# Two inputs of one stage laid side by side in DRAM: the first projection block of a hybrid mLSTM block

## Chip, cores, metric

The kernel runs on 1 core of one Trainium2 chip. The metric is the device time of one execution in microseconds (us). For the kernel before, 985.32 us is the median of 3 runs (985.29 to 987.55).

## What is computed

One layer of an encoder on x of shape (256 tokens, 2048 channels), float32. Cut to what matters here:

```python
h    = x * rsqrt(mean(x*x) + eps) * norm_pre_w
proj = h @ w_in                                   # 2048 x 16400, split into eleven parts:
q, k, v, o_g, z_a, i_pre, f_pre, u_b, z_b, g_a, g_b = split(proj)
# A: causal conv on q and k, SiLU, chunkwise mLSTM with 8 heads, per-head RMSNorm, gates o_g and z_a
# B: window means of u_b (windows 2, 4, 8, 16) minus u_b, a 256 x 256 map per group, gate z_b
merged = sigmoid(g_a) * (y_a @ w_proj_mlstm) + sigmoid(g_b) * (y_b @ w_proj_pool)
x + rmsnorm(merged @ w_out) * norm_post_w
```

## The kernel before, in words

All of it is matrix products on TensorE (PE) in a split precision: ScalarE (ACT) rounds a float32 tile to a high part (`hi`), VectorE (DVE) subtracts to get the low part (`lo`), and PE adds up hi·hi, lo·hi and hi·lo. The helper `hi_lo` (L56 to L65) issues both; L59 and L60 are the plain pair, L62 and L63 the pair that also multiplies by a scale per partition.

Weights stream from DRAM once. `w_tile` (L96) takes a 1 MB tile `raw` (128 partitions x 2048 floats, four k tiles of 512 columns), from the pool `rawp`, which has **three** such buffers for the whole kernel; SyncE (SP) issues the load, and `hi_lo` splits it into halves `wh`, `wl` (pool `split`, four of each). `tok_block` (L110) then multiplies: for each k tile of 128 channels, x's hi and lo (in `xc`, L89) stand still in PE, for two groups of 128 tokens, and 512 columns of `wh` or `wl` move: 6 matmuls per k tile, 96 in a block of 16 k tiles. `chan_block` (L131) does the same with the weights standing still; its matmuls are L142 and L144.

The change concerns the **first block** (`pu` of L410 with b = 0, the first 512 columns of u_b). Here x itself has still to be loaded and split, so the block is run with `first` (L207), which gives `w_tile` other cuts and a function `pre` that is called ahead of each cut. x lies in DRAM transposed (`xT`), with the norm weight ahead of it, as 16 floats per partition. For the first four k tiles (kq = 0) one k tile at a time comes, x by a transfer of 128 KB (136 KB with the norm weights) at L219 and the weights by one of 256 KB at L104; for the other twelve, two k tiles at a time, 256 KB of x and 512 KB of weights. x's tiles are `xt0` and two buffers `xt`, apart from `rawp`; a `raw` holds four k tiles of weights. All these transfers are in SP's queue, x and weights in turn.

Behind the first block stand, in the program: `stats` (L226), which loads x again by rows into two `raw` buffers (L231; called x0 and x1 below), squares and sums it on ACT (L232), from which DVE (L191) and GpSimd (POOL, L192) make `rstd`; `pooling` (L340), whose first step scales the block's result by `rstd` (`u_h`, `u_l`, L62 and L63); `stats_bc` (L237), which makes a diagonal matrix of `rstd` (`dg`, L241) and multiplies it by ones on PE (L242); and the block of z_b with two tiles `in_wq` (L100; t0 and t1 below). These are generators that `tok_block` and `chan_block` step once per half tile, and a scheduler orders each engine's instructions. `gates` loads `gw` (L249) and splits it into `gc` (L59 and L60).

Of the kernel before, what the change touches and what calls it, by code (L numbers as in the profile page):

```python
# [36 lines left out]
def block_kernel(ctx: ExitStack, tc: tile.TileContext, a: dict, out: bass.AP):  # L37
# [55 lines left out]
    def xl(k, t):  # L93
        return xc[:, k, 1, t * P : (t + 1) * P]

    def w_tile(src, cuts=(0, 1024, 2048), pre=None, pool=split):  # L96

        raw = rawp.tile([P, 2048], F32, name="raw")
        if pre is None:
            nc.sync.dma_start(raw, src)  # L100
        for c0, c1 in zip(cuts, cuts[1:]):
            if pre is not None:
                pre(c0)
                nc.sync.dma_start(raw[:, c0:c1], src[:, c0:c1])  # L104
            wh = pool.tile([P, 1024], F32R, name="wh")
            wl = pool.tile([P, 1024], F32R, name="wl")
            hi_lo(wh[:, : c1 - c0], wl[:, : c1 - c0], raw[:, c0:c1])
            yield c0, c1, wh, wl

    def tok_block(tiles, st_h, st_l, opts=lambda kq: {}):  # L110

        ps = [acc.tile([P, 512], F32, name="acc") for _ in range(2)]
        n = 4 * len(tiles)
        for kq, src in enumerate(tiles):
            for c0, c1, wh, wl in w_tile(src, **opts(kq)):
                for part in range(2):
# [12 lines left out]
        return ps
# [20 lines left out]
    def xtiles(b):  # L150
        return [a["wx"][b, i].rearrange("p k c -> p (k c)") for i in range(4)]
# [50 lines left out]
    pool_ctx = ExitStack()  # L202
    ph2 = pool_ctx.enter_context(tc.tile_pool(name="ph2", bufs=1, side="right"))
    sp = pool_ctx.enter_context(tc.tile_pool(name="start", bufs=1))
    xt0 = sp.tile([P, KT + 4 * T], F32, name="xt0")

    def first(kq):  # L207


        xt = xt0 if kq == 0 else sp.tile([P, KT + 4 * T], F32, name="xt", bufs=2)  # L210
        xk = xt[:, KT:].rearrange("p (k t) -> p k t", k=4)
        cuts = (0, 512, 1024, 1536, 2048) if kq == 0 else (0, 1024, 2048)

        def pre(c0):
            k0, k1 = c0 // 512, min(cc for cc in cuts if cc > c0) // 512
            s0, s1 = KT + k0 * T, KT + k1 * T
            if kq == 0 and k0 == 0:
                s0 = 0
            nc.sync.dma_start(xt[:, s0:s1], a["xT"][:, kq * 4 * T + s0 : kq * 4 * T + s1])  # L219
            for kk in range(k0, k1):  # L220
                k = kq * 4 + kk
                hi_lo(xc[:, k, 0], xc[:, k, 1], xk[:, kk], xt0[:, k : k + 1])

        return {"cuts": cuts, "pre": pre}

    def stats():  # L226

# [179 lines left out]
        yield 1  # L407

    for b in range(2):
        pu = tok_block(xtiles(12 + b), xh, xl, *([first] if b == 0 else []))  # L410
        if b == 0:
            side.append(gates())
        side.append(pooling(b, pu, zbs))
        for g in range(2 * b, 2 * b + 2):
            side.append(pool_gate(chan_block(qtiles(16 + g))))
# [157 lines left out]
    def st(tile_):  # L573
        return lambda k, t: tile_[:, k, t * P : (t + 1) * P]
# [138 lines left out]
def _per_channel(v):  # L713
    return v.reshape(-1, P).T
# [54 lines left out]
```

## Time and profile before

| | |
|---|---|
| median of 3 runs | 985.32 us |
| the profiled execution | 985.57 us, of it 983.8 us span |
| PE busy | 972.0 us (99%) |
| DVE, ACT busy | 626.5 us (64%), 481.7 us (49%) |
| moved by DMA | 188.45 MB, mean 192 GB/s |
| GB/s in the first three 24.6 us slices | 318, 320, 216 |

The span runs from the first to the last instruction. A group in the views has a line of the kernel, an engine, an operation and its tiles (out<-in). In a timeline, the first column is the start in us from the span's start, the second how long the row lasts, `x8` says how many instructions are in it, and the bracket gives the engine's idle time before it and what ended it. A matmul's duration overlaps the next one's; the distance between starts is what it costs. `SPq` rows are the issuing of a transfer, not the transfer.

### The profile page before, as it was taken

What the parts mean: (1) busy time and instruction counts of PE and PEld (TensorE: products, weight loads), DVE (VectorE), ACT (ScalarE), POOL (GpSimd) and SP (SyncE); (2) the same over time, 40 slices, a digit from 0 to 9 for tenths busy, and PEclk for the clock granted to TensorE, in tenths of its full rate; (3) what the DMA queues carried; (4) which work ended last, traced back from release to release, by engine and by line L of the source; (5) the groups of instructions that cost most, each with busy time, mean ns of one, the idle gap of its engine ahead of it and who ended that gap; (6) DMA issues with size and microseconds to landing.
All of it is one profiled execution on the core that took longest, in us unless ns stands there. A gap on an engine that the chain in (4) does not pass through costs nothing.

```text
span 983.8 us, 12219 instructions
## 1 busy us (share of the span) xinstructions
PE 972.0 (99%) x4777; PEld 819.4 (83%) x4777; DVE 626.5 (64%) x886; ACT 481.7 (49%) x614; POOL 14.3 (1%) x31
## 2 busy tenths in 40 slices
PE   9999999999999999999999999999999999999996
PEld 6788888888888888888888888888888888888886
DVE  7688747767767768668677586454454455454563
ACT  6746444446644465446544465434434434443451
POOL 1000000000000000000000000000000000000001
PEclk9999999999999999999999999999999999999999
DMA  9854455545364445464454554555556555567542
GB/s 318 320 216 171 152 191 194 192 160 188 130 244 178 172 171 176 167 219 166 171 191 168 199 194 149 196 194 192 189 173 212 187 198 177 209 236 272 181 166 86
DMA packets 29017, 188.45 MB, mean 192 GB/s; under 512 B 3232, under 2 KB 4000, under 8 KB 7200
## 3 DMA queue, kind: packets, MB, share of 16 engines
q1 hardware_dynamic: 28528, 184.53, 53.0%
q10 hardware_dynamic: 432, 3.15, 0.8%
q8 instruction: 37, 0.61, 0.2%
q14 instruction: 20, 0.16, 0.0%
HBM read 185.57 MB, written 2.10 MB: 191 GB/s over the span
## 4 chain that ended last, share of the span: by engine, by line
PE 96%; issue 1%; DMA 1%; ACT 0%; SPq 0%; POOL 0%; DVE 0%; DVEq 0%; ACTq 0%; POOLq 0%
PE acc L122 23%; PE acc L123 23%; PE acc L125 23%; PE acc L142 15%; PE acc L144 8%; PE sm L69 1%; PE sm L70 1%; PE sm L68 1%; DMA raw<-in_wx 1%; PE acc L68 0%; PE acc L70 0%; PE acc L69 0%; PE sm L266 0%; PE sm L579 0%; PE sm L533 0%
## 5 line engine op out<-in xcount | busy, mean ns | idle before, releaser
L60 DVE TENSOR_TENSOR wl<-raw,wh 128x1024 fp32r<-128x1024 f32 (+1 forms) x338 | 407.5, 1217 | 257.8 <-ACT wh L59 257.0
L59 ACT CAST wh<-raw 128x1024 fp32r<-128x1024 f32 (+1 forms) x338 | 350.8, 1046 | 393.0 <-PE acc L123 275.0
L122 PE MATMUL acc<-wh,xc 128*128 128x512 f32 x704 | 276.6, 393 | 1.0 <-ACT wh L59 1.0
L123 PE MATMUL acc<-wh,xc 128*128 128x512 f32 x704 | 274.7, 390 | 0.0
L125 PE MATMUL acc<-wl,xc 128*128 128x512 f32 x704 | 188.7, 389 | 0.0
L142 PE MATMUL acc<-xc,wh 128*128 128x512 f32 x640 | 160.7, 393 | 1.2 <-ACT wh L59 1.2
L122 PEld LDWEIGHTS acc<-wh,xc 128*128 128x128 f32 x704 | 132.5, 188 | 28.6 <-ACT wh L59 2.7
L125 PEld LDWEIGHTS acc<-wl,xc 128*128 128x128 f32 x704 | 132.2, 188 | 27.8
L123 PEld LDWEIGHTS acc<-wh,xc 128*128 128x128 f32 x704 | 132.6, 188 | 26.3
L142 PEld LDWEIGHTS acc<-xc,wh 128*128 128x128 f32 x640 | 115.9, 189 | 22.8 <-ACT wh L59 1.4
L144 PEld LDWEIGHTS acc<-xc,wl 128*128 128x128 f32 x640 | 87.3, 190 | 6.3
L144 PE MATMUL acc<-xc,wl 128*128 128x256 f32 x640 | 89.2, 282 | 0.0
L122 PE MATMUL acc<-wh,y_h 128*128 128x512 f32 x128 | 49.8, 389 | 0.0
L123 PE MATMUL acc<-wh,y_l 128*128 128x512 f32 x128 | 49.8, 389 | 0.0
L451 DVE SCALAR_TENSOR_TENSOR cy<-pad,vec,cy 128x256 f32<-128x256 f32 x96 | 39.4, 481 | 0.0
L122 PE MATMUL acc<-wh,m_h 128*128 128x512 f32 x96 | 37.6, 391 | 0.0
L123 PE MATMUL acc<-wh,m_l 128*128 128x512 f32 x96 | 37.4, 389 | 0.0
L125 PE MATMUL acc<-wl,y_h 128*128 128x512 f32 x128 | 34.2, 389 | 0.0
L393 DVE TENSOR_REDUCE pad<-acc 128x256 f32<-128x512 f32 x32 | 20.6, 686 | 14.6 <-PE acc L144 14.6
L123 PEld LDWEIGHTS acc<-wh,y_l 128*128 128x128 f32 x128 | 24.0, 188 | 5.0
L125 PEld LDWEIGHTS acc<-wl,y_h 128*128 128x128 f32 x128 | 24.0, 188 | 5.0
L122 PEld LDWEIGHTS acc<-wh,y_h 128*128 128x128 f32 x128 | 24.0, 188 | 5.0
(188 smaller groups left out, 757.2 us busy)
## 6 DMA issues: line engine op xcount, KB each, us to landing
raw<-in_wx SPq DMA_DIRECT2D x84, 1024.0 KB, 4.8
raw<-in_wq SPq DMA_DIRECT2D x40, 1024.0 KB, 4.8
raw<-in_wpm SPq DMA_DIRECT2D x16, 1024.0 KB, 4.9
raw<-in_wo SPq DMA_DIRECT2D x16, 1024.0 KB, 5.0
raw<-in_wpp SPq DMA_DIRECT2D x8, 1024.0 KB, 4.8
raw<-in_wx SPq DMA_DIRECT2D x6, 512.0 KB, 6.9
raw<-in_x SPq DMA_DIRECT2D x2, 1024.0 KB, 7.7
xr<-in_x ACTq DMA_DIRECT2D x2, 1024.0 KB, 7.1
```

The source lines that it names most:

```text
L59: nc.scalar.copy(hi, src)
L60: nc.vector.tensor_tensor(lo, src, hi.bitcast(F32), op=ALU.subtract)
L68: nc.tensor.matmul(ps, lh, rh, start=start, stop=False)
L69: nc.tensor.matmul(ps, ll, rh, start=False, stop=False)
L70: nc.tensor.matmul(ps, lh, rl, start=False, stop=stop)
L122: nc.tensor.matmul(ps[t], st_h(k, t), wh[:, cols], start=k == 0, stop=False)
L123: nc.tensor.matmul(ps[t], st_l(k, t), wh[:, cols], start=False, stop=False)
L125: nc.tensor.matmul(ps[t], st_h(k, t), wl[:, cols], start=False, stop=k == n - 1)
L142: nc.tensor.matmul(ps[c], wh[:, cols], xc[:, k], start=k == 0, stop=False)
L144: nc.tensor.matmul(ps[c][:, 1], wl[:, cols], xc[:, k, 0], start=False, stop=k == KT - 1)
L393: nc.vector.tensor_reduce(dst, ps.rearrange("p a b -> p b a"), axis=AX.X, op=ALU.add)
L451: nc.vector.scalar_tensor_tensor(y, pad[:, 1 + j : 1 + j + T], cw[:, j : j + 1], y, op0=ALU.mult, op1=ALU.add)
```

## The change

x (256 floats per partition and k tile) and the weights of the first block (512 floats) are put side by side in one DRAM array `xw`, 3 KB per partition and k tile, the norm weights ahead of them as before. A transfer brings x and weights of one k tile, one k tile, two k tiles, and from then on of two at a time: 384, 384 and 768 KB. Only the first k tile comes in two transfers (136 KB with x, 256 KB with weights) into a buffer of its own, `xw0`. All others go into `raw` buffers, of which a transfer of two k tiles fills three quarters. The two buffers `xt` are gone. `w_tile` loses its options. The block's columns leave the array `wx`, whose later blocks move up by one.

```diff
+XW = T + 512
...
-    def w_tile(src, cuts=(0, 1024, 2048), pre=None, pool=split):
+    def w_tile(src, pool=split):
 
         raw = rawp.tile([P, 2048], F32, name="raw")
-        if pre is None:
-            nc.sync.dma_start(raw, src)
-        for c0, c1 in zip(cuts, cuts[1:]):
-            if pre is not None:
-                pre(c0)
-                nc.sync.dma_start(raw[:, c0:c1], src[:, c0:c1])
+        nc.sync.dma_start(raw, src)
+        for c0, c1 in ((0, 1024), (1024, 2048)):
...
-    def tok_block(tiles, st_h, st_l, opts=lambda kq: {}):
+    def tok_block(tiles, st_h, st_l, load=w_tile):
...
-            for c0, c1, wh, wl in w_tile(src, **opts(kq)):
+            for c0, c1, wh, wl in load(src):
...
-    xt0 = sp.tile([P, KT + 4 * T], F32, name="xt0")
+    xw0 = sp.tile([P, KT + XW], F32, name="xw0")
 
     def first(kq):
-        xt = xt0 if kq == 0 else sp.tile([P, KT + 4 * T], F32, name="xt", bufs=2)
-        xk = xt[:, KT:].rearrange("p (k t) -> p k t", k=4)
-        cuts = (0, 512, 1024, 1536, 2048) if kq == 0 else (0, 1024, 2048)
-
-        def pre(c0):
-            k0, k1 = c0 // 512, min(cc for cc in cuts if cc > c0) // 512
-            s0, s1 = KT + k0 * T, KT + k1 * T
-            if kq == 0 and k0 == 0:
-                s0 = 0
-            nc.sync.dma_start(xt[:, s0:s1], a["xT"][:, kq * 4 * T + s0 : kq * 4 * T + s1])
-            for kk in range(k0, k1):
-                k = kq * 4 + kk
-                hi_lo(xc[:, k, 0], xc[:, k, 1], xk[:, kk], xt0[:, k : k + 1])
-
-        return {"cuts": cuts, "pre": pre}
+        for k0, n in ((0, 1), (1, 1), (2, 2)) if kq == 0 else ((0, 2), (2, 2)):
+            c0 = KT + (kq * 4 + k0) * XW
+            if c0 == KT:
+                for s0, s1 in ((0, KT + T), (KT + T, KT + XW)):
+                    nc.sync.dma_start(xw0[:, s0:s1], a["xw"][:, s0:s1])
+                raw = xw0[:, KT:]
+            else:
+                raw = rawp.tile([P, 2048], F32, name="raw")[:, : n * XW]
+                nc.sync.dma_start(raw, a["xw"][:, c0 : c0 + n * XW])
+            r = raw.rearrange("p (k c) -> p k c", k=n)
+            wh = split.tile([P, 1024], F32R, name="wh")
+            wl = split.tile([P, 1024], F32R, name="wl")
+            w = [p[:, : n * 512].rearrange("p (k c) -> p k c", k=n) for p in (wh, wl)]
+            for kk in range(n):
+                k = kq * 4 + k0 + kk
+                hi_lo(xc[:, k, 0], xc[:, k, 1], r[:, kk, 0:T], xw0[:, k : k + 1])
+            hi_lo(*w, r[:, :, T:XW])
+            yield k0 * 512, (k0 + n) * 512, wh, wl
...
-        pu = tok_block(xtiles(12 + b), xh, xl, *([first] if b == 0 else []))
+        pu = tok_block(range(4), xh, xl, first) if b == 0 else tok_block(xtiles(12), xh, xl)
...
-        "xT": np.concatenate(
-            [_per_channel(g["norm_pre_w"][0]), x.reshape(T, KT, P).transpose(2, 1, 0).reshape(P, KT * T)], axis=1
-        ),
+        "xw": np.concatenate([_per_channel(g["norm_pre_w"][0]), xw.reshape(P, KT * XW)], axis=1),
```

In SP's queue at the start of the program, before: x and weights in turn; from row to row only the DMAHW numbers (transfers that must have landed) and one DVE wait tell when a row may go.

```order
L219 DMA xt_129<-in_xT 128x272
L104 DMA raw<-in_wx 128x512
...
L219 DMA xt<-in_xT 128x512 [waits DMAHW0_49]
L104 DMA raw<-in_wx 128x1024 [waits DMAHW1_49]
...
L219 DMA xt<-in_xT 128x512 [waits DMAHW2_49,DMAHW0_49,DVE_49]
L104 DMA raw<-in_wx 128x1024 [waits DMAHW1_49]
...
L100 DMA raw<-in_wq 128x2048 [waits DMAHW4_49,DVE_49]
L249 DMA gw<-in_wg 128x256 [waits DMAHW5_49]
...
L231 DMA raw<-in_x 128x2048 [waits DMAHW0_49,DVE_49]
L231 DMA raw<-in_x 128x2048 [waits DMAHW3_49,DMAHW1_49,DVE_49]
```

The same queue in the changed kernel (`in_xw` is the joint array; rows of the first block in order k tile 0 in two transfers, 1, 2 and 3, 4 and 5, ...):

```order
L211 DMA xw_129<-in_xw 128x272
L211 DMA xw_129<-in_xw 128x512
L215 DMA raw<-in_xw 128x768
L215 DMA raw<-in_xw 128x1536 x2
L215 DMA raw<-in_xw 128x1536 [waits DMAHW2_49,DVE_49]
L249 DMA gw<-in_wg 128x256
L215 DMA raw<-in_xw 128x1536 [waits DMAHW3_49,DVE_49]
L215 DMA raw<-in_xw 128x1536 [waits DMAHW4_49,DMAHW0_49,DVE_49]
...
L100 DMA raw<-in_wq 128x2048 [waits DMAHW0_49,DVE_49]
L252 DMA vec<-in_vecs 128x184
L231 DMA raw<-in_x 128x2048 [waits DMAHW6_49,DMAHW1_49,DVE_49]
L231 DMA raw<-in_x 128x2048 [waits DMAHW3_49,DVE_49]
```

Twenty rows of the first block have become ten; five go without a wait, and every later one waits for DVE, which has to be done with the `raw` buffer that the row fills again. The load of `gw` has moved from behind t0 (`in_wq`) into the block.

On ACT the splitting of `gw` has moved too. In the changed kernel it stands between the pieces for k tiles 6 and 7 and those for 8 and 9 (`xc` is x's part, `wh` the weights'):

```order
L63 ACTIVATE xc<-raw,xw_129 128x256 [waits DMAHW5_49]
L63 ACTIVATE xc<-raw,xw_129 128x256
L60 CAST wh<-raw 128x1024 [waits DVE_49,PE_49]
L60 CAST gc<-gw 128x4x2x8 [waits DMAHW6_49]
L60 CAST gc<-gw 128x4x2x8 x3
L63 ACTIVATE xc<-raw,xw_129 128x256 [waits DMAHW7_49]
```

Before, it stood behind the first block and both halves of t0, just ahead of the squares of x0. Otherwise ACT's, DVE's and PE's instructions are the same ones in the same order, with k tiles 2 and 3 now taken together on all three.

## Rows read from the trace of the kernel before

**Rows 1.** The page's part 1: busy us of each engine, its share of the span, and its instructions.

```profile
PE 972.0 (99%) x4777; PEld 819.4 (83%) x4777; DVE 626.5 (64%) x886; ACT 481.7 (49%) x614; POOL 14.3 (1%) x31
```

**Rows 2.** The waits of PE in the whole span, those for data: line waited for, us in total, times, longest.

```profile
PE acc L142 <- ACT wh L59: 1.2, 1, 1.2
PE acc L122 <- ACT wh L59: 1.0, 2, 0.8
```

**Rows 3.** Timeline of PE at the start: the warm-up matmuls, then first matmuls of k tiles 1, 2, 3, of the pairs 4 and 5, 6 and 7, and 8 and 9.

```profile
1.19 4.02 PE L165 MATMUL sm<-zeros 128*128 128x512 bf16 x9 [1.19 <-DVE zeros L160]
...
7.16 0.39 PE L122 MATMUL acc<-wh,xc 128*128 128x512 f32 x1
...
8.52 0.39 PE L122 MATMUL acc<-wh,xc 128*128 128x512 f32 x1
...
10.30 0.50 PE L122 MATMUL acc<-wh,xc 128*128 128x512 f32 x1 [0.26 <-ACT wh L59]
...
12.74 0.50 PE L122 MATMUL acc<-wh,xc 128*128 128x512 f32 x1 [0.77 <-ACT wh L59]
...
15.59 0.39 PE L122 MATMUL acc<-wh,xc 128*128 128x512 f32 x1
...
18.31 0.39 PE L122 MATMUL acc<-wh,xc 128*128 128x512 f32 x1
```

**Rows 4.** Timeline of PE behind the first block: start of t0, its last group, the two diagonal products, start of t1.

```profile
29.19 1.98 PE L142 MATMUL acc<-xc,wh 128*128 128x512 f32 x8
...
33.80 1.11 PE L144 MATMUL acc<-xc,wl 128*128 128x256 f32 x8
35.54 0.71 PE L242 MATMUL sm<-dg,ones_f 128*128 128x128 f32 x4 [0.63 <-DVE dg L241]
37.45 2.12 PE L142 MATMUL acc<-xc,wh 128*128 128x512 f32 x8 [1.20 <-ACT wh L59]
```

**Rows 5.** Timeline of ACT in the same stretch.

```profile
27.12 0.68 ACT L59 CAST gc<-gw 128x64 fp32r<-128x64 f32 x4
28.19 1.92 ACT L232 ACTIVATE raw<-raw 128x2048 f32<-128x2048 f32 x1 [0.39 <-DMA raw<-in_x]
...
32.17 1.92 ACT L232 ACTIVATE raw<-raw 128x2048 f32<-128x2048 f32 x1 [1.97 <-DMA raw<-in_x]
33.99 0.18 ACT L232 ACTIVATION_READ_ACCUMULATOR raw<-raw 128x1 f32 x1
35.20 1.26 ACT L62 ACTIVATE u_h<-acc,rstd 128x512 fp32r<-128x512 f32 x2 [1.02 <-POOL rstd L192]
36.35 4.11 ACT L59 CAST wh<-raw 128x1024 fp32r<-128x1024 f32 x4
```

**Rows 6.** Timeline of DVE: the low part of the last pair of k tiles, 14 and 15, of the first block.

```profile
23.80 1.22 DVE L60 TENSOR_TENSOR wl<-raw,wh 128x1024 fp32r<-128x1024 f32 x1 [1.23 <-ACT wh L59]
```

**Rows 7.** Timeline of ACT at the start: weights of k tile 0, x of k tile 1, x and weights of k tiles 4 and 5.

```profile
4.44 0.62 ACT L59 CAST wh<-raw 128x512 fp32r<-128x512 f32 x1 [0.95 <-DMA raw<-in_wx]
4.97 0.50 ACT L62 ACTIVATE xc<-xt 128x256 fp32r<-128x256 f32 x1
...
10.27 0.91 ACT L62 ACTIVATE xc<-xt,xt 128x256 fp32r<-128x256 f32 x2
11.64 1.05 ACT L59 CAST wh<-raw 128x1024 fp32r<-128x1024 f32 x1 [0.46 <-DMA raw<-in_wx]
```

**Rows 8.** Timeline of SP's issues: x and weights of k tile 0, weights of k tile 3, weights of 10 and 11, then x0 (the x2 row merges it with x1), and x1 alone.

```profile
0.74 0.39 SPq L219 DMA_DIRECT2D xt<-in_xT  x1
1.18 0.42 SPq L104 DMA_DIRECT2D raw<-in_wx  x1
...
4.01 0.43 SPq L104 DMA_DIRECT2D raw<-in_wx  x1
...
9.62 0.33 SPq L104 DMA_DIRECT2D raw<-in_wx  x1
...
19.79 5.59 SPq L231 DMA_DIRECT2D raw<-in_x  x2
25.06 0.33 SPq L231 DMA_DIRECT2D raw<-in_x  x1
```

**Rows 9.** DMA issues taken one at a time by narrow stretches: KB, and us from the start of the issue to landing. In order: the six issues of the group before (0.74, 1.18, 4.01, 9.62, 19.79 and 25.06 us), and the load of `pw` at 39.95 us, when little else was on its way.

```profile
xt<-in_xT SPq DMA_DIRECT2D x1, 136.0 KB, 2.2
raw<-in_wx SPq DMA_DIRECT2D x1, 256.0 KB, 3.2
raw<-in_wx SPq DMA_DIRECT2D x1, 256.0 KB, 5.6
raw<-in_wx SPq DMA_DIRECT2D x1, 512.0 KB, 7.7
raw<-in_x SPq DMA_DIRECT2D x1, 1024.0 KB, 8.4
raw<-in_x SPq DMA_DIRECT2D x1, 1024.0 KB, 7.0
raw<-in_pw SPq DMA_DIRECT2D x1, 1024.0 KB, 4.7
```

**Rows 10.** Busy time by stretch (us PE, PEld, DVE, ACT, POOL; then granted clock, DMA share, GB/s), 4 to 8 us.

```profile
4.00:6.00 2.00, 2.00 (x5) 0.94 (x4) 0.92 (x3) 1.03 (x2) 0.00 (x0) 1.00 0.95 260
6.00:8.00 2.00, 2.00 (x9) 1.62 (x9) 1.28 (x4) 1.72 (x4) 0.00 (x0) 1.00 1.07 295
```

More of the change, by code (lines that the diff above doesn't have):

```diff
@@ L94, in xl @@
         return xc[:, k, 1, t * P : (t + 1) * P]
-    def w_tile(src, cuts=(0, 1024, 2048), pre=None, pool=split):
+    def w_tile(src, pool=split):
         raw = rawp.tile([P, 2048], F32, name="raw")
-        if pre is None:
-            nc.sync.dma_start(raw, src)
-        for c0, c1 in zip(cuts, cuts[1:]):
-            if pre is not None:
-                pre(c0)
-                nc.sync.dma_start(raw[:, c0:c1], src[:, c0:c1])
+        nc.sync.dma_start(raw, src)
+        for c0, c1 in ((0, 1024), (1024, 2048)):
             wh = pool.tile([P, 1024], F32R, name="wh")
             wl = pool.tile([P, 1024], F32R, name="wl")
-            hi_lo(wh[:, : c1 - c0], wl[:, : c1 - c0], raw[:, c0:c1])
+            hi_lo(wh, wl, raw[:, c0:c1])
             yield c0, c1, wh, wl
-    def tok_block(tiles, st_h, st_l, opts=lambda kq: {}):
+    def tok_block(tiles, st_h, st_l, load=w_tile):
         ps = [acc.tile([P, 512], F32, name="acc") for _ in range(2)]
@@ L590, in block_kernel @@
         for n in range(2):
-            pg = tok_block(xtiles(14 + 4 * n + j), xh, xl)
+            pg = tok_block(xtiles(13 + 4 * n + j), xh, xl)
             for t in range(2):
@@ L661, in block_kernel @@
     for j in range(3):
-        po = tok_block(otiles(j), st(m_h), st(m_l), lambda kq: {"pool": osplit})
+        po = tok_block(otiles(j), st(m_h), st(m_l), lambda src: w_tile(src, osplit))
         for t in range(2):
@@ L724 @@
     cw = g["qk_conv_w"][0].reshape(4, 32, P).transpose(2, 1, 0).reshape(P, 128)
+    xw = np.concatenate(
+        [x.reshape(T, KT, P).transpose(2, 1, 0), w_in[:, 10256:10768].reshape(KT, P, 512).transpose(1, 0, 2)], axis=2
+    )
     arrays = {
         "x": x,
-        "xT": np.concatenate(
-            [_per_channel(g["norm_pre_w"][0]), x.reshape(T, KT, P).transpose(2, 1, 0).reshape(P, KT * T)], axis=1
-        ),
+        "xw": np.concatenate([_per_channel(g["norm_pre_w"][0]), xw.reshape(P, KT * XW)], axis=1),
         "vecs": np.ascontiguousarray(
@@ L745 @@
         "wx": np.concatenate(
-            [_tiles(w_in[:, c0:c1], 512, 4) for c0, c1 in ((4096, 10240), (10256, 11280), (12304, 16400))]
+            [_tiles(w_in[:, c0:c1], 512, 4) for c0, c1 in ((4096, 10240), (10768, 11280), (12304, 16400))]
         ),
```

## The prediction, as put on record

> **What bounds the kernel now.** I read the busy times first, then PE's waits, then the timelines of the first 40 us of PE, ACT, SP and the DMA landings. PE is busy for 972.0 us of a span of 983.8 [rows 1]. Its waits for data are few, and all stand at the start: 1.0 us for the split weights of the first block, and 1.2 us at the second tile of the next block [rows 2]. The reader should see that the change touches 40 us of 985, and in them at most a few us.
>
> Within these 40 us there are two losses. The first is in the first block itself. Twelve matmuls of two k tiles take 2.72 us when nothing is missing (15.59 to 18.31), six take 1.36 (7.16 to 8.52). From k tile 2 at 8.52 the pair 6 and 7 would be reached 2 x 1.36 + 2.72 = 5.44 us later, at 13.96; it starts at 15.59. So 1.6 us are lost there, waiting for weights [rows 3]. The second loss is behind the block: t0 ends at 33.80 + 0.95 = 34.75 and t1 starts at 37.45; two small products of some 0.5 us lie between [rows 4], so 2.2 us are lost.
>
> The second is the one that counts. ACT works in order: the weights of t1 (36.35) stand behind `u_h` (35.20), which needs `rstd`, which needs the square of x1 (32.17), which waits for x1's load [rows 5]. x1 was issued at 25.06 and landed 7.0 us later, at 32.06 [rows 8, 9]. From that landing to t1's start are 37.45 - 32.06 = 5.4 us of a fixed chain. And x1 was issued at 25.06 because DVE let go of the buffer at 23.80 + 1.22 = 25.02 [rows 6]. Hence t1's start is the later of two times: x1's landing plus 5.4 us, or the end of PE's own work, which was ready 2.2 us earlier. **Time that PE gains or loses in the first block is taken up in that slack; only x1's landing moves the end.** Behind t1 PE waits for no data [rows 2], so a shift there reaches the end.
>
> **The change, part by part.** PE's instructions, ACT's and DVE's splits and the bytes are the same; only when things land differs. So I walk the landings through the first block, with these prices.
>
> - Data of a transfer after another that keeps the queue full: weights of k tile 3 land at 4.01 + 5.6 = 9.61, those of 10 and 11 at 9.62 + 7.7 = 17.32; 8 k tiles of 384 KB between them, 3.15 MB in 7.71 us, 408 GB/s. Two k tiles (768 KB) then take 1.93 us, 1 MB takes 2.57 [rows 8, 9].
> - From issue to the first data: 136 KB took 2.2 us and 1 MB 4.7 us with little beside them, so 364 GB/s between and 1.8 us ahead of the data [rows 9].
> - ACT: x of two k tiles 0.91, weights 1.05, together 1.96 us; for one k tile 0.50 and 0.62 [rows 7]. DVE is done some 1.25 us behind ACT, as its row of 1.22 us says [rows 6].
>
> The unknown is the rate at the start. Before, x of k tile 0 lands at 0.74 + 2.2 = 2.94 and the weights of k tile 3 at 9.61: 1.44 MB in 6.67 us, 216 GB/s, far under 408 [rows 8, 9]. The bytes moved in 4 to 8 us are 260 and 295 GB/s [rows 10]. Whether pieces of 3 and 6 KB per partition mend this, no row shows: 216 bounds it below, 408 above. I take 278, the mean of the two stretches, since these are what the transfers did in just this time, whoever's bytes they were, and use 408 from k tile 4 on.
>
> Weights of k tile 0 land as now at 1.18 + 3.2 = 4.38. k tile 1 then lands at 5.8 (0.39 MB at 278), k tiles 2 and 3 at 8.6, 4 and 5 at 10.55. Those three fill the three `raw` buffers. From here on a load goes only when DVE has finished with a buffer, which is new: before, the loads of twelve k tiles went with no wait for DVE.
>
> - k tile 1: ACT done at 6.9, DVE at 7.6, so 6 and 7 are issued; their data could come at 9.45, but follow 4 and 5: landed 12.5.
> - 2 and 3: ACT done 10.6, DVE 11.8; 8 and 9 issued, data at 13.6. The queue ran empty at 12.5: **1.1 us of nothing**. Landed 15.55.
> - 4 and 5: DVE 13.8; 10 and 11 land at 17.5. 6 and 7: DVE 15.75; 12 and 13 land at 19.5.
> - 8 and 9: ACT 17.5, DVE 18.8; 14 and 15 issued, data at 20.6, again 1.1 us of nothing, landed 22.5.
> - 10 and 11: DVE 20.7; t0 lands 25.1. 12 and 13: DVE 22.7; x0 lands at 25.1 + 2.57 and the small `vec`, 27.9 (now 19.79 + 8.4 = 28.19).
> - 14 and 15: ACT 24.5, DVE 25.7: x1 is issued, 0.7 us later than now.
>
> x1's landing: now it comes 32.06 - 28.19 = 3.87 us behind x0 [rows 8, 9]; at 408 GB/s it would be 2.57, and by its own 7.0 us from the issue it would be 32.7. So 30.5 to 32.7, and I take 3.87, the row for just this transfer: 31.8. t1 starts at 31.8 + 5.4 = 37.2, against 37.45: **-0.25 us**.
>
> PE meanwhile: k tile 1 at 7.16 as now, done 8.5. k tiles 2 and 3 start only when both are split, at 10.6: a gap of 2.1 us, in place of gaps of 0.4 and 1.0 now. From there seven pairs run without a wait (each is split before its turn; 4 and 5 at 12.5 for 13.3, 8 and 9 at 17.5 for 18.8): 10.6 + 7 x 2.72 = 29.65, 0.45 us later than now. t0 adds 5.56: 35.2, with the small products 35.7, still 1.5 us ahead of 37.2. PE's lateness is hidden by the wait for x1; without that cover it would cost 0.45 us.
>
> The split of `gw`, 0.68 us on ACT [rows 5], moves into the block, into ACT's idle time from 14.5 to 15.55; its load (128 KB, behind 6 and 7) has landed by 13. Where it stood ACT waits for x0 anyway. Nothing. Fewer issues on SP, five without a wait instead of eight: nothing, since DMA and not SP is late after 4 us. The later blocks of `wx` lie elsewhere in DRAM: nothing that a row could price.
>
> Sum: the profiled execution took 985.57 us, 0.25 more than the median; -0.25 gives 985.3, and on the median's scale 985.32 - 0.25, **985.1**, a shift that no measurement of this kernel tells from none (about 0.3%, 3 us; the three runs differ by 2.3).
>
> **Rivals.**
>
> *The start runs at full rate.* If larger pieces bring 408 GB/s from k tile 1 on, k tiles 1, 2 and 3, 4 and 5 land at 5.3, 7.3 and 9.2; the walk then gives x1's issue at 25.0, and, behind an x0 at 27.2, 2.57 us later, its landing at 29.8. t1 starts at 35.2: -2.25, 983.1 us. For it: the later pieces of 2 and 4 KB go at 408. Against it: the two empty stretches stay, and x1's 3.87 us were not made by small pieces. To pass 0.3% x1 would have to land before 29.1. Chance 0.20. The Trainium skill, "DMA: Bandwidth & Descriptors", section "Rules for kernel authors", says the same in its own terms: coalesce many small transfers into large ones, at least 1 MiB each for the best rate. By that rule this rival's 983.1 would be the result; the trace agrees as far as its slowest stretch, 216 GB/s, is that of the smallest transfers.
>
> *Three buffers are too few, and x1 comes late.* This is the one on the other side. If the start stays at 216 GB/s, k tile 1 lands at 6.2, 2 and 3 at 9.85, 8 and 9 at 16.8, 14 and 15 at 23.7, and x1 is issued at 26.95. By its row of 7.0 us it lands at 33.95, t1 starts at 39.35: +1.9, 987.2 us; by x0's 8.4 us it would be +3.3, 988.6. It decides from the moment that x1 lands behind 32.06, and passes 0.3% behind 35.0. For it: every load waits for DVE now, and x needs its weights to have landed too, so ACT can no longer split x ahead as it does at 4.97 [rows 7]. Against it: x1's 7.0 us contained x0's last 3 us, which are the same bytes. Chance 0.20. The same section of the Trainium skill's page says to issue a DMA early and wait for it late, and from k tile 6 on the change issues every load of the block later than now. By that rule this rival's 987.2 would be the result; no row of before shows a first block with so short a lead.
>
> *PE slows down in its gap.* The nine warm-up matmuls take 4.02 us, 0.43 us each, 512 columns at the 1.2 GHz level; later ones are 0.227 us apart, the 2.4 GHz level [rows 3]. If 2.1 us without work brought the low level back for 4 us, 1.9 us would go, PE would be done at 37.6 instead of 35.7, 0.4 behind x1's chain: 985.4. After the gap of 1.0 us at 12.74 the level stayed. Chance 0.04.
>
> **The numbers.** Forecast 0.56, within 1.2 us of no change; full rate 0.20; late x1 0.20; slow PE 0.04. Beyond 0.3% lie a fifth of the first rival (0.04) and a quarter of the second (0.05): faster 0.04, same 0.91, slower 0.05. The range takes in the bounds of both unknowns, the start's rate and x1's landing: 982.9 to 987.5.
>
> **What would show it.** Right: x1 issued at 25 to 27 us, landed at 30.5 to 33; t1's first matmul 5.4 us later; a PE gap of about 2 us ahead of k tiles 2 and 3, and none in the rest of the block; two stretches of about 1 us with little DMA, near 13 and 20 us. Wrong: t1 starting right behind t0 (then PE's stream is the bound, and the first block's gaps count); a PE gap at every pair (the buffers starve PE); matmuls 0.43 us apart behind 8 us; or a difference that arises behind 60 us, of which this working has none.

## The result, and the profile after

The changed kernel takes **991.0 us** (median of 6 runs, 989.26 to 992.5) where the kernel before, beside it, takes 985.74 (6 runs): ratio **1.0045 [1.0034, 1.0056]**. With the experiments it ran once more: 990.5 (12 runs) against 986.3, 1.0036 [1.0024, 1.0048]. So it is slower, by 3.5 to 4.4 us going by the ratios and by 4.2 to 5.3 us between the medians; it lies outside the range (982.9 to 987.5) and on the side that had a chance of 0.05. The profiled execution took 989.26 us with a span of 987.5, which is 3.7 us more than the 983.8 of before; where these 3.7 us lie is read below.

Lines have moved: PE's L122, L123 and L125 of before are L119, L120 and L122 now, L142 and L144 are L139 and L141, ACT's L59 and L62 are L60 and L63, DVE's L60 is L61. The page's part 1 answers to [rows 1]:

```profile
PE 973.6 (99%) x4777; PEld 820.2 (83%) x4777; DVE 626.5 (63%) x885; ACT 481.1 (49%) x613; POOL 14.3 (1%) x31
```

The same 4777 matmuls keep PE busy 1.6 us longer: some of them ran slower. The rest is waiting. PE's waits for data in the whole span, as [rows 2]:

```profile
PE sm L242 <- DVE dg L241: 2.0, 1, 2.0
PE acc L119 <- ACT wh L60: 1.6, 1, 1.6
PE acc L139 <- ACT wh L60: 1.5, 2, 1.2
```

All lie in the first 40 us, as before. PE's timeline, as [rows 3, 4]: first matmuls of k tile 1, of k tiles 2 and 3, the end of the first block, t0, the diagonal products, t1.

```profile
6.93 0.50 PE L119 MATMUL acc<-wh,xc 128*128 128x512 f32 x1
...
10.19 0.50 PE L119 MATMUL acc<-wh,xc 128*128 128x512 f32 x1 [1.60 <-ACT wh L60]
...
28.63 1.07 PE L122 MATMUL acc<-wl,xc 128*128 128x512 f32 x4
30.00 2.11 PE L139 MATMUL acc<-xc,wh 128*128 128x512 f32 x8 [0.30 <-ACT wh L60]
...
34.74 1.11 PE L141 MATMUL acc<-xc,wl 128*128 128x256 f32 x8
37.85 0.71 PE L242 MATMUL sm<-dg,ones_f 128*128 128x128 f32 x4 [2.00 <-DVE dg L241]
39.76 3.68 PE L139 MATMUL acc<-xc,wh 128*128 128x512 f32 x8 [1.20 <-ACT wh L60]
43.27 1.13 PE L141 MATMUL acc<-xc,wl 128*128 128x256 f32 x8
```

Two things are to be seen. t1 starts at 39.76, **2.31 us later** than at 37.45 [rows 4]. And its first eight matmuls take 43.27 - 39.76 = 3.51 us up to the next group, where the eight of t0 take 1.95 (30.00 to 31.95): **1.55 us more**. Together 3.86, against 3.7 in the span. The slow ones ran at the lower clock level, as the busy time by stretch says (columns as in [rows 10]: PE to POOL, then granted clock, DMA share, GB/s):

```profile
37.00:40.00 3.00, 0.95 (x5) 0.76 (x6) 2.25 (x6) 2.49 (x4) 0.48 (x1) 0.98 0.90 333
40.00:43.00 3.00, 3.00 (x8) 2.32 (x8) 3.00 (x3) 2.67 (x4) 0.00 (x0) 0.50 0.56 232
```

0.50 is the 1.2 GHz level; before, the same stretch stood at 1.00:

```profile
40.00:43.00 3.00, 3.00 (x20) 2.67 (x19) 2.19 (x2) 1.84 (x2) 0.00 (x0) 1.00 0.66 199
```

Ahead of the fall PE had only the two diagonal products to do, from the end of t0 at 35.7 to 39.76.

t1 is late for the reason that the prediction's chain names. ACT, as [rows 5] (squares of x0 and x1, `u_h`, the weights of t1):

```profile
31.61 1.92 ACT L232 ACTIVATE raw<-raw 128x2048 f32<-128x2048 f32 x1 [0.71 <-DMA raw<-in_x]
...
34.48 1.91 ACT L232 ACTIVATE raw<-raw 128x2048 f32<-128x2048 f32 x1 [0.87 <-DMA raw<-in_x]
...
37.51 1.26 ACT L63 ACTIVATE u_h<-acc,rstd 128x512 fp32r<-128x512 f32 x2 [1.02 <-POOL rstd L189]
38.66 3.99 ACT L60 CAST wh<-raw 128x1024 fp32r<-128x1024 f32 x4
```

The square of x1 waits for its load, which came 2.3 us later than in [rows 5]. From the landing at 34.42 to t1 are 5.34 us; the prediction's fixed chain had 5.4.

Why the load came late stands in its queue. SP's issues, as [rows 8]: `gw`, then k tiles 8 to 13 (three issues at 11.42, 13.35 and 16.07 in one row), 14 and 15, t0, then x0 and x1 in one row:

```profile
8.00 0.43 SPq L249 DMA_DIRECT2D gw<-in_wg  x1
11.42 4.98 SPq L215 DMA_DIRECT2D raw<-in_xw  x3
...
18.96 0.35 SPq L215 DMA_DIRECT2D raw<-in_xw  x1
22.33 0.33 SPq L100 DMA_DIRECT2D raw<-in_wq  x1
...
25.20 2.25 SPq L231 DMA_DIRECT2D raw<-in_x  x2
```

and each one's way from issue to landing, taken one at a time as in [rows 9]; in order k tiles 8 and 9, 10 and 11, 12 and 13, 14 and 15, t0, x0, x1 (x1 issued at 27.12):

```profile
raw<-in_xw SPq DMA_DIRECT2D x1, 768.0 KB, 4.4
raw<-in_xw SPq DMA_DIRECT2D x1, 768.0 KB, 5.8
raw<-in_xw SPq DMA_DIRECT2D x1, 768.0 KB, 6.0
raw<-in_xw SPq DMA_DIRECT2D x1, 768.0 KB, 4.9
raw<-in_wq SPq DMA_DIRECT2D x1, 1024.0 KB, 6.5
raw<-in_x SPq DMA_DIRECT2D x1, 1024.0 KB, 6.3
raw<-in_x SPq DMA_DIRECT2D x1, 1024.0 KB, 7.3
```

The landings are then 15.8, 19.15, 22.07, 23.86, 28.83, 31.5 and 34.42; k tiles 6 and 7, issued at 7.63, landed at 12.93. With never more than two or three loads on their way, 768 KB came 2.9, 3.3 and 2.9 us behind the 768 KB ahead of them, not 1.93; only k tiles 14 and 15 came 1.8 us behind. The start was faster than before, though; the rows answer to [rows 10]:

```profile
4.00:6.00 2.00, 2.00 (x6) 1.19 (x5) 0.85 (x2) 0.76 (x2) 0.00 (x0) 1.00 1.00 336
6.00:8.00 2.00, 1.94 (x9) 1.27 (x8) 1.18 (x2) 0.88 (x2) 0.00 (x0) 1.00 0.99 396
...
12.00:14.00 2.00, 2.00 (x11) 1.65 (x10) 1.84 (x4) 1.06 (x3) 0.00 (x0) 1.00 0.82 204
14.00:16.00 2.00, 2.00 (x11) 1.65 (x10) 1.55 (x3) 1.54 (x6) 0.00 (x0) 1.00 1.05 335
16.00:18.00 2.00, 2.00 (x10) 1.69 (x9) 1.67 (x8) 1.68 (x3) 0.00 (x0) 1.00 0.96 316
18.00:20.00 2.00, 2.00 (x10) 1.65 (x9) 1.20 (x2) 0.81 (x2) 0.00 (x0) 1.00 0.85 313
```

336 and 396 GB/s where [rows 10] have 260 and 295; but then 204 to 335, where the kernel before moves 406 and 364:

```profile
10.00:14.00 4.00, 2.97 (x12) 2.10 (x12) 2.77 (x5) 3.46 (x7) 0.00 (x0) 1.00 1.03 406
14.00:18.00 4.00, 4.00 (x19) 3.33 (x18) 4.00 (x7) 3.86 (x7) 0.00 (x0) 1.00 1.00 364
```

The DMA share, the figure ahead of the GB/s, stays at 0.82 to 1.05 in the slow rows: for the most part the engines count as busy and move less, rather than standing empty. From 16 to 20 us the two kernels differ little (332 and 341 GB/s before, behind a wait of its own: it issues no load from 9.62 to 14.77 us); from 20 to 24 us it is 310 and 174 against 391.

### The profile page after: what moved, and what is told of

The parts are those of the page before. It is cut to its first block, busy times and chain, and to the rows that moved or that the text cites. A ratio compares the mean times of both kernels' runs of the same rounds, so it can differ in the third digit from the quotient of the medians.

```text
span 987.5 us, 12207 instructions
## 1 busy us (share of the span) xinstructions
PE 973.6 (99%) x4777; PEld 820.2 (83%) x4777; DVE 626.5 (63%) x885; ACT 481.1 (49%) x613; POOL 14.3 (1%) x31
## 4 chain that ended last, share of the span: by engine, by line
PE 94%; DMA 2%; issue 1%; ACT 1%; DVE 1%; POOL 0%; SPq 0%; DVEq 0%; POOLq 0%; ACTq 0%
PE acc L119 22%; PE acc L120 22%; PE acc L122 22%; PE acc L139 15%; PE acc L141 8%; DMA raw<-in_xw 2%; PE sm L70 1%; PE sm L71 1%; PE sm L69 1%; DMA raw<-in_x 1%; PE acc L71 0%; PE acc L69 0%; PE acc L70 0%; PE sm L266 0%; PE sm L579 0%
## 5 line engine op out<-in xcount | busy, mean ns | idle before, releaser
L61 DVE TENSOR_TENSOR wl<-raw,wh 128x1024 fp32r<-128x1024 f32 (+1 forms) x336 | 406.2, 1220 | 255.9 <-ACT wh L60 255.7
L60 ACT CAST wh<-raw 128x1024 fp32r<-128x1024 f32 (+1 forms) x336 | 349.8, 1049 | 389.3 <-PE acc L120 275.1
L119 PE MATMUL acc<-wh,xc 128*128 128x512 f32 x704 | 276.7, 393 | 1.7 <-ACT wh L60 1.6
L120 PE MATMUL acc<-wh,xc 128*128 128x512 f32 x704 | 274.6, 390 | 0.0
L122 PE MATMUL acc<-wl,xc 128*128 128x512 f32 x704 | 188.5, 389 | 0.0
L139 PE MATMUL acc<-xc,wh 128*128 128x512 f32 x640 | 162.4, 396 | 1.5 <-ACT wh L60 1.5
L119 PEld LDWEIGHTS acc<-wh,xc 128*128 128x128 f32 x704 | 132.5, 188 | 29.4 <-ACT wh L60 3.3
L122 PEld LDWEIGHTS acc<-wl,xc 128*128 128x128 f32 x704 | 132.1, 188 | 27.8
L120 PEld LDWEIGHTS acc<-wh,xc 128*128 128x128 f32 x704 | 132.4, 188 | 26.1
L139 PEld LDWEIGHTS acc<-xc,wh 128*128 128x128 f32 x640 | 116.8, 190 | 23.8 <-ACT wh L60 2.1
L141 PEld LDWEIGHTS acc<-xc,wl 128*128 128x128 f32 x640 | 87.5, 191 | 6.4
L141 PE MATMUL acc<-xc,wl 128*128 128x256 f32 x640 | 89.2, 282 | 0.0
L119 PE MATMUL acc<-wh,y_h 128*128 128x512 f32 x128 | 49.8, 389 | 0.0
L120 PE MATMUL acc<-wh,y_l 128*128 128x512 f32 x128 | 49.8, 389 | 0.0
L119 PE MATMUL acc<-wh,m_h 128*128 128x512 f32 x96 | 37.6, 391 | 0.0
L120 PE MATMUL acc<-wh,m_l 128*128 128x512 f32 x96 | 37.4, 389 | 0.0
L122 PE MATMUL acc<-wl,y_h 128*128 128x512 f32 x128 | 34.2, 389 | 0.0
L119 PEld LDWEIGHTS acc<-wh,y_h 128*128 128x128 f32 x128 | 24.0, 188 | 5.0
L122 PEld LDWEIGHTS acc<-wl,y_h 128*128 128x128 f32 x128 | 24.0, 188 | 5.0
L120 PEld LDWEIGHTS acc<-wh,y_l 128*128 128x128 f32 x128 | 24.0, 188 | 5.0
```

The source lines that it names most:

```text
L122: nc.tensor.matmul(ps[t], st_h(k, t), wl[:, cols], start=False, stop=k == n - 1)
L139: nc.tensor.matmul(ps[c], wh[:, cols], xc[:, k], start=k == 0, stop=False)
L141: nc.tensor.matmul(ps[c][:, 1], wl[:, cols], xc[:, k, 0], start=False, stop=k == KT - 1)
```

## The experiments

**Theory A**: the three `raw` buffers now hold x as well as weights, so a load is issued only when DVE is done with an older one; with so few loads on their way each lands late, x1 last, and t1 waits for it; the gap that opens also lets the clock fall. **Theory B**: the joint transfers themselves are to blame. **Theory C**: the moved `gw`. Ratios are against the kernel before, run beside each; its median was 987.0, 986.3 and 986.45 us in the three sessions (e1 to e4; e5a, e5b, e6 and the repeat; e7 to e9).

### The changed kernel once more

Unchanged, beside e5 and e6.

> The changed kernel once more, unaltered, beside the runs of the kernel before that the next three share. Both theories: 3 to 6 us above the kernel before; t1 starts at 39 to 41 us, and low clock (matmuls 0.43 us apart) shows in the first matmuls of t1, or in k tiles 2 to 5 behind PE's gap, or in both.

Measured: ratio 1.0036 [1.0024, 1.0048], 986.5 to 991.51 us; in its profile (span 987.6) t1 starts at 39.87 and the next group 2.94 us later, with the clock at 0.60 from 40 to 43 us. Same place, same two terms.

### e1: two transfers get room of their own

k tile 1 and k tiles 2 and 3 go into tiles of their own, so the three `raw` buffers begin with k tile 4.

```diff
-                raw = rawp.tile([P, 2048], F32, name="raw")[:, : n * XW]
+                if kq == 0:
+                    raw = sp.tile([P, n * XW], F32, name=f"xw{k0}")
+                else:
+                    raw = rawp.tile([P, 2048], F32, name="raw")[:, : n * XW]
```

> The joint layout and its transfers are kept, but k tile 1 and k tiles 2 and 3 get buffers of their own, so that the three raw buffers first serve k tiles 4 to 9: two more loads go without waiting for DVE. Theory A (three raw buffers are too few: loads are issued late, x1 lands late, PE waits ahead of t1 long enough for its clock to fall): x1 lands at 30 to 32.5 us instead of 34.4, t1 starts at 36 to 38 us instead of 39.8, no matmul of t1 is slow, 984 to 986.5 us. Theory B (the joint transfers themselves are to blame: x comes only with its weights, and big pieces land later): x1 still lands behind 34 us, 989 to 991.5 us.

Measured: 988.5 us, ratio 1.002 [1.001, 1.0031], about half of the changed kernel's loss; span 985.8. The queue moved 399 and 421 GB/s from 8 to 12 us, with the same transfers, then ran dry: after `gw` at 4.14 no load is issued until 13.42 us, and the bytes fall to 155 GB/s. x1 landed at 33.7 and t1 started at 39.09, between what A and what B expected: the lead was used up by the time the ring began to turn. The clock fell here too, but in another place:

```profile
10.00:12.00 2.00, 1.74 (x5) 1.41 (x6) 1.76 (x3) 1.98 (x4) 0.00 (x0) 0.67 1.01 421
12.00:14.00 2.00, 2.00 (x7) 1.51 (x6) 2.00 (x4) 1.93 (x4) 0.00 (x0) 0.50 0.41 155
```

That is behind the gap ahead of k tile 2; t1's first eight took 2.11 us. There the loss is covered by the wait for x1. The 399 and 421 GB/s speak against B; for A the run alone does not decide.

### e2: the kernel before, with a buffer per pair of k tiles

The separate transfers stay, but a `raw` now holds the weights of two k tiles in place of four: as short a ring as the change has.

```diff
-        raw = rawp.tile([P, 2048], F32, name="raw")
         if pre is None:
+            raw = rawp.tile([P, 2048], F32, name="raw")
             nc.sync.dma_start(raw, src)
...
             if pre is not None:
+                if c0 % 1024 == 0:
+                    raw = rawp.tile([P, 2048], F32, name="raw")
                 pre(c0)
```

> The kernel before, x and weights in separate transfers as there, but each pair of k tiles of weights takes a raw buffer of its own (half filled), so the three buffers hold six k tiles of weights instead of twelve. Theory A: the loads of weights wait for DVE from k tile 6 on, x1 lands 1 to 3 us later than 32.06, t1 starts at 38.5 to 40.5 us and its first matmuls are slow: 987.5 to 992 us. Theory B: separate transfers are what was good, so 985.3 to 986.3 us as before.

Measured: 989.05 us, ratio 1.0024 [1.0015, 1.0033], span 986.5. x1 landed at 33.2, t1 started at 38.63, and the clock fell at t1:

```profile
36.72 0.71 PE L244 MATMUL sm<-dg,ones_f 128*128 128x128 f32 x4 [2.37 <-DVE dg L243]
38.63 3.31 PE L144 MATMUL acc<-xc,wh 128*128 128x512 f32 x8 [1.20 <-ACT wh L59]
```

The old transfers, with the ring alone shortened, show a late t1 (1.2 us of the change's 2.3) and the same fall of the clock in the same place. That speaks for A. The other half of the delay is not in this run, in which x still has buffers of its own and does not share the ring.

### e3: PE kept busy ahead of t1

The changed kernel with 13 products of zeros, made to wait for ACT's sums and for `rstd`, between t0 and t1.

```diff
+        fill = small()
+        for scale, count in ((sums0[0][:, 0:1], 9), (rstd[:, 0:1], 4)):
+            z = sp.tile([P, P], BF16, name="z", bufs=2)
+            nc.gpsimd.tensor_scalar(z, zeros[:, 0:P], scale, None, op0=ALU.mult)
+            for _ in range(count):
+                nc.tensor.matmul(fill, z, zeros, start=True, stop=True)
```

> The changed kernel with 13 matmuls of zeros on PE in the wait ahead of t1 (nine behind t0, made to wait for the sum of x0's squares, four behind the diagonal products); nothing else changes. If the clock's fall in the gap is a loss of its own: x1 lands and t1 starts as in the changed kernel (34.4, 39.8 us), the first eight matmuls of t1 take 2.0 us instead of 3.7, the granted clock stays at 1.00, and the time falls by 1.5 to 3.5 us to 987.5 to 989.5. If the slow matmuls are something else (contention while t1 starts): no gain, 990.5 to 991.5.

Measured: 989.5 us, ratio 1.0023 [1.0013, 1.0032]. In the profiled execution (span 988.0) t1's first eight took 2.11 us at full clock:

```profile
39.48 1.03 PE L247 MATMUL sm<-zeros,z 128*128 128x512 bf16 x4
40.76 2.11 PE L139 MATMUL acc<-xc,wh 128*128 128x512 f32 x8 [0.25 <-ACT wh L60]
```

But the clock had fallen behind k tile 2 this time (0.50 from 12 to 14 us), the block ran late, x1 came at 35.4 and t1 at 40.76; a later wait took 0.8. The shift of t1, 3.3, and 0.8 give the 4.2 of the span. The ratio is lower than the change's (1.0036 and 1.0045, in other sessions; its interval overlaps that of the first and not that of the second), which fits a clock term of one or two us; the profile can't show it, since this execution lost by the clock elsewhere.

### e4: gw's load and split back behind t0

```diff
-        gw = sp.tile([P, KT, 2, NH], F32, name="gw")
+        gw = sp.tile([P, KT + XW], F32, name="xw0")[:, : KT * 16].rearrange("p (k g h) -> p k g h", k=KT, g=2)
```

> The changed kernel with gw in a buffer that comes free only behind the first block (xw0's), so its load and its split stand behind t0 again on SP, ACT and DVE, as in the kernel before. Theory C (gw's load and split inside the block delay DVE, and with it the release of buffers): x1 lands about 1 us earlier or more, 988.5 to 990 us. Theory A alone: within 0.7 us of the changed kernel, 990.3 to 991.7.

Measured: 989.51 us, ratio 1.0028 [1.0018, 1.0038], span 987.6; t1 at 39.90, its first eight slow (3.68 us), x1 landed at 34.6, as in the changed kernel. The median lies in C's range, but the kernel before beside it was 1.3 us slower than in the first session, and the trace is against C: with no `gw` in the block, the loads of k tiles 8 to 15 were issued at 11.60, 13.53, 15.78 and 19.02 us, as in the changed kernel (11.42, 13.35, 16.07 and 18.96), and 14 and 15 landed later (24.8 for 23.86). So the move of `gw` makes neither the late x1 nor the fall. The edit is not clean behind the block: SP waits 3.9 us for the buffer of `gw`, and x0's load, next in the queue, goes out at 26.69 in place of 25.20.

### e5a, e5b, e6: a buffer for every transfer

If A holds, the cure is to give every transfer of the first block its own buffer. A pool `xwp` that is closed behind the block, before `ph2` opens, has the room. e5a does it for the joint transfers, e6 in the same way for the separate ones of before, e5b is e5a with k tiles 2 and 3 in a transfer each.

```diff
+    xw_ctx = ExitStack()
+    xwp = xw_ctx.enter_context(tc.tile_pool(name="xwp", bufs=1, side="right"))
...
-                raw = rawp.tile([P, 2048], F32, name="raw")[:, : n * XW]
+                raw = xwp.tile([P, n * XW], F32, name=f"xw{kq * 4 + k0}")
...
+    pu0 = tok_block(range(4), xh, xl, first)
+    xw_ctx.close()
+    pool_ctx = ExitStack()
```

e5b also:

```diff
-        for k0, n in ((0, 1), (1, 1), (2, 2)) if kq == 0 else ((0, 2), (2, 2)):
+        for k0, n in ((0, 1), (1, 1), (2, 1), (3, 1)) if kq == 0 else ((0, 2), (2, 2)):
```

> The joint layout and the same transfers, but every transfer of the first block has a buffer of its own, in a pool that is closed before the pooling branch's pool is opened; no load of the block, of t0, x0 or x1 waits for DVE. Theory A (the ring of three raw buffers): x1 lands at 26 to 30 us, t1 starts as soon as PE is through with t0, at 35 to 36.5 us, and the time is 0.5 to 2.5 us under the kernel before; the gap of 2 us ahead of k tiles 2 and 3 stays, with low clock behind it in some runs. Theory B (the joint transfers themselves): x1 behind 32 us, 1.5 us or more above the kernel before.

> As the kernel before this one, with k tiles 2 and 3 in a transfer each. Theory A: PE's gap ahead of k tile 2 shrinks from 2 us to under 1, no low clock behind it, t0 ends at 32.5 to 34 us and t1 starts at 33 to 35 us: 2.5 to 4 us under the kernel before. Theory B: no better than the kernel before.

> The kernel before, with x and weights in separate transfers as there, but with buffers of their own for all of the first block. Theory A: x1 lands at 27 to 30 us, t1 starts right behind t0 at 35 to 36 us: 1.5 to 2.5 us under the kernel before, and above the one with joint transfers one by one, since the pieces of the first four k tiles land more slowly. Theory B: this one is the best of the three with buffers of their own.

Measured: e5a 983.79 us, ratio 0.9972 [0.9962, 0.9983]; e5b 983.56 us, 0.9969 [0.9958, 0.9981]; e6 984.1 us, 0.9972 [0.9961, 0.9984]. All three beat both kernels. In e5a the loads are all issued by 6.70 us, t0's at 6.75, x0's and x1's from 14.43:

```profile
1.64 5.06 SPq L214 DMA_DIRECT2D xw<-in_xw  x8
6.75 0.44 SPq L100 DMA_DIRECT2D raw<-in_wq  x1
...
14.43 2.21 SPq L236 DMA_DIRECT2D raw<-in_x  x2
```

and the same 768 KB transfers go at 421 and 432 GB/s where the changed kernel has 204 to 335:

```profile
12.00:16.00 4.00, 4.00 (x20) 3.27 (x19) 3.98 (x7) 3.98 (x7) 0.00 (x0) 1.00 1.01 421
16.00:20.00 4.00, 4.00 (x19) 3.32 (x18) 4.00 (x8) 3.93 (x7) 0.00 (x0) 1.00 1.03 432
```

x1's square starts at 29.36, and t1 follows t0 with no wait:

```profile
34.38 1.11 PE L141 MATMUL acc<-xc,wl 128*128 128x256 f32 x8
35.33 0.60 PE L247 MATMUL sm<-dg,ones_f 128*128 128x128 f32 x4
35.69 2.09 PE L139 MATMUL acc<-xc,wh 128*128 128x512 f32 x8
```

Now PE's own stream is the bound, and the gap ahead of k tile 2 (1.64 us in e5a, at 10.58) counts; e5b brings k tile 2 at 8.69, with gaps of 0.50 and 0.61, and t1 at 34.78, 0.9 earlier, though the medians (983.79 and 983.56) lie too close to tell apart. e6 is as good as e5a: with room for every transfer, joining them is worth nothing that can be measured, though the start is faster with the joint ones (336 and 363 GB/s from 4 to 8 us in e5a, 237 and 307 in e6). B is out on both sides.

### e7: both gaps filled

e3 with 8 more products of zeros ahead of k tile 2, waiting for the split x of k tile 1.

```diff
+            if kq == 0 and k0 == 2:
+                z1 = sp.tile([P, P], BF16, name="z1")
+                nc.gpsimd.tensor_scalar(z1, zeros[:, 0:P], xc[:, 1, 1, 0:1].bitcast(F32), None, op0=ALU.mult)
+                fill1 = small()
+                for _ in range(8):
+                    nc.tensor.matmul(fill1, z1, zeros, start=True, stop=True)
```

> The changed kernel with products that fill both gaps of PE: 8 products with zeros ahead of k2 and 13 ahead of t1. If the clock's fall in one or the other gap is a part of the loss beside the late x1 (theory A with its clock term), no stretch of the first 45 us after the warm-up stays at 1.2 GHz, t1 starts at 39.5 to 40.8 us as in the changed kernel, its first eight matmuls take 2.1 us, and the span is over the kernel before by the shift of t1 alone, 2 to 3.3 us (ratio 1.002 to 1.0033). If the late t1 is the whole of it (rival), the clock makes no difference and the ratio is 1.004 as for the changed kernel; if the clock is the whole of it, the ratio is 1.000.

Measured: 989.65 us, ratio 1.0044 [1.0027, 1.006]. The eight runs fall in two groups: five from 989.13 to 989.71 with a mean granted clock of 0.998 or 0.999 over the span, three from 992.16 to 993.23 at 0.997. The profiled one is of the second group: nothing fell in the first block, but x1 landed at 36.1, 2.11 us were still empty ahead of t1, and the clock fell there.

```profile
41.42 3.14 PE L139 MATMUL acc<-xc,wh 128*128 128x512 f32 x8 [2.11 <-ACT wh L60]
44.37 1.67 PE L141 MATMUL acc<-xc,wl 128*128 128x256 f32 x8
```

The expectation for t1 and for its first eight is missed in this execution. The first group's median, 989.44, is 3.0 us over the median of the kernel before beside it (986.45), and 4.0 us over that of the nine of its runs with the same mean clocks (0.998 and 0.999; 985.47). t1 came 4.0 us late here (41.42 for 37.45), so a late t1 alone would cost as much; that group has no profile, so this is a reading of its times. The ratio lies where the expectation put it if the late t1 is the whole of the loss, but it can't decide that, since t1 is 1.7 us later than in the changed kernel. Filling PE does not give the loss back, since x1 stays late.

### e8, e9: a fourth raw buffer

The changed kernel (e8) and the kernel before (e9), with one number changed.

```diff
-    rawp = ctx.enter_context(tc.tile_pool(name="rawp", bufs=3, side="right"))
+    rawp = ctx.enter_context(tc.tile_pool(name="rawp", bufs=4, side="right"))
```

> The changed kernel with four raw buffers in place of three. Theory A (x1 is late since the ring gives back buffers late): each load of the first block is issued one buffer earlier, more of them are outstanding at once, x1 lands 1.5 to 4 us earlier than the 34.4 us of the changed kernel, t1 starts at 36 to 38.4 us, and the ratio is 0.999 to 1.002. Theory B (the joint transfers are slow by themselves): x1 within 0.5 us of 34.4 and the ratio 1.0035 to 1.005.

> The kernel before with four raw buffers. Theory A: the kernel before is itself held by its three buffers, though less, so x1 lands 1 to 3 us earlier than at 32.1 us, t1 starts at 35.6 to 36.8 us, and the ratio is 0.9972 to 0.999. If the kernel before is not held by them (rival), the ratio is 1.000 and t1 stays at 37.4 us.

Measured: e8 985.92 us, ratio 0.9995 [0.9985, 1.0006]; e9 987.56 us, 1.001 [0.9999, 1.0022]. In e8 x1 lands at 30.27 and t1 starts at 35.63, 4.1 us earlier than in the changed kernel, earlier than expected, and as early as with a buffer for each of the same transfers (e5a):

```profile
35.63 2.11 PE L139 MATMUL acc<-xc,wh 128*128 128x512 f32 x8 [0.56 <-ACT wh L60]
```

One buffer more is enough to undo the late t1. In e8 `gw` is back behind t0 too, which by e4 does not matter. In e9 x1 lands at 31.0, t1 at 36.30, 1.15 earlier than before, as A has it. The times don't show it in full, since a fourth buffer moved the order of a late stage: eight small products (L579) now stand ahead of a block in place of within it, and PE waits for their input in both kernels. In e8:

```profile
887.28 1.23 PE L579 MATMUL sm<-ident,g 128*128 128x128 f32 x8 [1.84 <-DVE g L613]
```

and behind this wait the clock falls once more:

```profile
888.00:890.00 2.00, 2.00 (x9) 1.66 (x9) 2.00 (x2) 2.00 (x3) 0.00 (x0) 0.68 1.01 426
890.00:892.00 2.00, 2.00 (x6) 1.52 (x6) 2.00 (x4) 2.00 (x4) 0.00 (x0) 0.50 1.01 426
```

Four microseconds at 0.68 and 0.50 lose 2 x 0.32 + 2 x 0.50 = 1.6 us of full clock. So in e8 -1.82 at t1, +1.84 and +1.6 make +1.6, against +1.7 in its span of 985.5; in e9 -1.15, +1.85 and 2 x (0.18 + 0.50 + 0.17) = 1.7 make +2.4, against +2.6. e9's ratio missed its expectation for this reason, not by its start.

## Why the prediction was wrong

**The frame held.** "Only x1's landing moves the end": it landed at 34.42, t1 came 5.34 us later, and nothing behind 45 us waits. PE did have one gap of 1.6 to 2 us, ahead of k tiles 2 and 3 at 10.19 (10.6 was forecast), and none in the rest of the block. k tiles 2 and 3 landed at 8.3 and 4 and 5 at 10.1 (8.6 and 10.55 forecast): the rate at the start, held to be the unknown, was if anything better than the 278 GB/s taken. `gw` cost nothing (e4).

**The step that failed** is the price of a load once the ring turns: 1.8 us to the first data and then 408 GB/s, 1.93 us per 768 KB. That rate was read from a stretch of before in which the queue was kept full [rows 8, 9], and put on a ring that keeps one to three loads on their way. The walk then has 1.95 and 2.0 us between landings that follow one another, and two stretches of 1.1 us with nothing, near 13 and 20 us. Measured: landings 2.9, 3.3 and 2.9 us apart, and no empty stretch near 20 us (DMA share 0.85 and 0.92 from 18 to 22 us). The walk was on time up to k tiles 8 and 9 (15.8 for 15.55), then slipped: 10 and 11 at 19.15 for 17.5, 12 and 13 at 22.07 for 19.5, 14 and 15, which came at the price, at 23.86 for 22.5. The largest slip is t0's: DVE let go of its buffer late, it was issued at 22.33 for 20.7 and took 6.5 us, 4.4 by the walk, so it landed at 28.83 for 25.1, and x0 behind it at 31.5 for 27.9. DVE was done with the last at 27.10 as its row says,

```profile
25.88 1.22 DVE L61 TENSOR_TENSOR wl<-raw,wh 128x1024 fp32r<-128x1024 f32 x1
```

so x1 was issued at 27.12 in place of 25.7, and took 7.3 us, 1.2 more than the walk gave it. e5a shows that it is not their shape: the same transfers, all issued ahead, go at 421 and 432 GB/s. Why fewer loads on their way move fewer bytes while the engines count as busy no run shows. The Trainium skill, "DMA: Bandwidth & Descriptors", section "Rules for kernel authors", asks for loads issued early and waited for late as much as for large ones; the runs agree with the first by the whole loss and more (the same transfers issued early, e5a, 0.9972, against the change beside it, 1.0036: 6.3 us), and with the second by nothing that can be measured (e5a against e6, both 0.9972).

**The rival that came true** is the late x1 (0.20): it put t1 at 39.35 and the time at 987.2, and t1 did start at 39.76. Its condition was wrong, a start at 216 GB/s; the late x1 came with a start faster than the forecast's, from the short queue, so that its 39.35 fits so well is luck. The late x1 should have been the forecast, and its "against" (x1's 7.0 us held x0's last bytes) weighed too much.

**The term that was missing** is the clock in the gap ahead of t1. A fall to 1.2 GHz was considered only in the first block's gap, priced as covered, and given 0.04 since the level stayed after a gap of 1.0 us. It fell where there is no cover: 1.55 us at t1. That is the sign of being wrong that the prediction named, matmuls 0.43 us apart behind 8 us: t1's first eight start 0.44 us apart (3.51 us). The term is read from the traces; e3 and e7, meant to take it away alone, lost by the clock elsewhere (e3) or in the same place (e7), so that the gap is what lets the clock fall is argued, not shown. In the first gap the clock may fall too (e1, e3); in e1 it is covered there by the wait for x1.

The sum with these sizes is 2.31 + 1.55 = 3.86 for the 3.7 of the profiled spans. The medians differ by more, 5.3 us. The profiled execution is the fastest of its six and the one with a mean clock of 0.995; the other five have 0.994 and 990.1 to 992.5 us. One part in a thousand of 990 us is 1 us, so a longer or second fall could make most of it; those executions have no profile, and this stays open.

One sum of the prediction does not follow from its own walk, that of the start at full rate. With k tiles 2 and 3 landing 1.3 us earlier than in the forecast, every later step moves by 1.3 us: x1 is issued at 24.4 and not 25.0 and lands at 29.2, t1 starts at 34.6, and the time is 982.4, outside the range, in place of 983.1.

## What to carry to other kernels

Before transfers are joined, count how many buffers they then share: a ring that is refilled only when the consumer lets go sets how many loads are on their way, and a rate read from a full queue does not hold in a short one. Follow the last load of the stage, not the first: what was gained at the start was lost a few loads later. And a wait on TensorE is to be priced with the slow matmuls behind it, wherever it is not covered by a later wait.

## What the runs showed that was not expected

- **The rate goes with the number of loads on their way.** The same 768 KB transfers went at 204 to 335 GB/s with at most three under way (12 to 20 us of the changed kernel), at 286 to 375 with a fourth buffer (e8), and at 421 and 432 with all issued ahead (e5a).
- **The clock's fall varies from execution to execution of one program.** In the profiles it follows the gap ahead of t1 (changed kernel, e2, e4, e7), that ahead of k tile 2 (e1, e3), or one at 887 us (e8, e9), each with an idle stretch of 1.8 to 2.4 us in it. It doesn't follow every such gap: 2.1 us ahead of k tile 2 passed without it in e4. The kernel before itself ran from 984.24 to 989.03 us in the last session, with mean clocks from 0.999 to 0.994. The Trainium skill, "TensorE: Matmul & The Clock Gate", section "What's actually happening", calls the number of slow matmuls at a kernel's start variable from run to run; e7's two groups, 989.4 and 992.5 us, fit such a variation in mid-kernel too.
